# Start addresses and block sizes of the moving operands in a two-chunk encoder layer

## The chip, the cores and the metric

The kernel runs on one core of a Trainium2 chip. The metric is the device time of one launch in microseconds; the median of the runs counts. The core's engines are called as in the profile: PE (TensorE, with PEld for its weight loads), DVE (VectorE), ACT (ScalarE), POOL (GpSimd) and SP (SyncE, which here issues every DMA).

## What is computed

One layer of a hybrid encoder is applied to two sequences, a prompt of 1024 tokens and a sample of 256. Sixteen meta tokens stand ahead of each. The model width is 2048, and a head has 128 numbers. Cut to what matters:

```python
def encoder_layer(h, ...):                       # h: meta tokens, then the sequence
    u = rms_norm(h, norm_w) @ w_in               # 2048 -> 6656 = 52 strips of 128
    qa, ka, va, za, qb, kb, vb, zb = split(u)
    qa, ka = rope(rms_norm(qa)), rope(rms_norm(ka))
    ya = global_gqa(qa, ka, va) * silu(za)       # 8 heads, 2 key heads, all tokens
    qb, kb = rms_norm(qb), rms_norm(kb)
    yb = neighbourhood_attention(qb, kb, vb, rpb) * silu(zb)   # 8 heads, local windows + meta keys
    return h + concat([ya, yb]) @ w_out          # 2048 -> 2048

y_prompt, y_sample = encode(x_prompt), encode(x_sample)        # without the meta rows
```

Everything is float32.

## The kernel before

**Operands.** Each float32 operand of a projection is split into a rounded half h (float32r) and the remainder l. A product then takes three matmuls: wh with xh, wh with xl, wl with xh. Weights are the stationary operand (128x128), tokens are the moving one. A tile of moving tokens has shape `[P, 2, T]`: h in `t[:, 0, :]`, l right behind it in `t[:, 1, :]`.

**Two chunks of tokens.** Chunk 1 holds T1 = 512 tokens: 16 meta tokens, the 256 of the sample, and the first C1P = 240 of the prompt, in this order. Chunk 2 holds the T2 = 784 other prompt tokens. For each chunk, 52 strips of `w_in` (128 output columns each) are multiplied with 16 k-tiles of tokens (`strips`, lines 196 to 198). A strip of chunk 1 is one block: all 512 tokens for k and v (`B0`), and 496 for q and z (`BQ`), which need no meta tokens and so start at token 16. A strip of chunk 2 is two blocks of 392 tokens (`BL`, line 662).

**Around the strips.** After each strip an evacuation reads PSUM: `qk_evac` (norm, rope and split), `z_evac` (silu), or `v_rows` with `rows_out`, where TensorE turns v to token-major form, 128 tokens at a time, ACT copies it and SP stores it. Attention is interleaved: `attend` (L318 to 320 and L358 to 361) for global heads, `attend_sample` and `attend_strip` for local ones. k, v, q and z of chunk 1's prompt part pass through DRAM (`kd`, `vn`, `qd`, `zd`) and are loaded in chunk 2. A scheduler sets the order of instructions when the kernel is built; DMAs all go through SP's queue.

**Out projection.** `outproj` multiplies `w_out` with TH = 640 columns at a time, in seven products instead of eight, formed from sums of operand quarters. Each is two blocks of 320 columns of a tile `ym`, shape `[P, 2, 640]` (`products`, lines 913 to 915).

**Memory.** A DMA scratch of 16384 bytes a partition stands at the bottom of SBUF, below the kernel's tiles. The tiles x and ym start at 96 past a multiple of 128 bytes. A second half starts 2048 bytes behind the first in chunk 1, 3136 in chunk 2 and 2560 in the out projection; the second block starts 1568 bytes in (chunk 2) or 1280 (out projection).

Of the kernel before, what the change touches and what calls it, by code (L numbers as in the profile page):

```python
# [20 lines left out]
P = 128  # L21
# [8 lines left out]
T2 = NP - C1P  # L30
NH = 8
# [14 lines left out]
class Kern:  # L46
# [88 lines left out]
    def load_all_x(self):  # L135


        nc = self.nc
        t = [self.x.tile([P, 2, T2], F32R, tag="x", name="x") for _ in range(KT)]
        for kt, i in enumerate((3, 4, 0, 1, 2, *range(5, KT))):  # L140
            h, l = t[i][:, 0, :], t[i][:, 1, :]
            r = l.bitcast(F32)
            with self.tc.issue_after(self.early):
                nc.sync.dma_start(r, self.x2d[kt][:])
            w = self.nw[:, kt:kt + 1]
            nc.scalar.activation(h, r, AF.Copy, scale=w)
# [217 lines left out]
    def attend_sample(self, q, zs, k, meta, vals, vmeta, tab, ydst):  # L364
# [123 lines left out]
    def copy_km(self, k):  # L488

        km = self.k.tile([P, 2, 3, NMETA], F32R, tag="km", name="km")  # L490
        self.nc.scalar.copy(km[:], k[:, :, :NMETA].bitcast(F32).unsqueeze(2).to_broadcast([P, 2, 3, NMETA]))
        km = km[:].rearrange("p i c m -> p i (c m)")
        return km[:, 0], km[:, 1]
# [58 lines left out]
    def chunk1(self):  # L552
# [21 lines left out]

        def v_strip(s, g):
# [4 lines left out]
            def evac(ps):  # L580
                vt = self.v_rows(ps[0], *B0)
                self.split(vm[:, 0:1, :], vm[:, 1:2, :], self.v_turn(vt, [0], NMETA))
                if loc:
                    nc.scalar.copy(vs[:], self.v_turn(vt, [NMETA + 32 * w0 for w0 in WIN0]))
                else:
                    self.split(vs[:, :2, :], vs[:, 2:, :], self.v_turn(vt, [NMETA, NMETA + P]))
                self.rows_out(vt[:, PS:], C1P, self.vn[g], 0)
# [5 lines left out]
        def q_strip(s, h, wc, rope):  # L593
            q = self.s.tile([P, 2, QB], F32R, tag="S", name="qs")

            def evac(ps):
                o, n = BQ
                qp = [self.ev.tile([P, C1P], F32R, tag="ev", name="qp") for _ in range(2)]
                self.qk_evac(ps[0], o, n, wc, (ct[:, o:], st[:, o:]) if rope else None,
# [16 lines left out]
        def run(h, q, z, k, v, vm, tab):  # L616
# [5 lines left out]
            o = NMETA  # L622
            keys = [(k[:, 0, o + P * j:o + P * j + P], k[:, 1, o + P * j:o + P * j + P]) for j in range(2)]
# [29 lines left out]
    def chunk2(self):  # L653
# [8 lines left out]
        BL = [(0, T2 // 2), (T2 // 2, T2 // 2)]  # L662
# [3 lines left out]
        def k_first(g):  # L666
            k = self.k.tile([P, 2, NMETA + NP], F32R, tag="k1", name="kf")
            nc.sync.dma_start(k[:, :, :K0].bitcast(F32), self.kd[g][:])
            return k, self.copy_km(k)
# [169 lines left out]
    def y_load(self, p, k):  # L839
# [6 lines left out]
        if p in (1, 2, 4):  # L846
            t = self.ym.tile([P, 2, TH], F32R, tag="ym", name="ym")
# [5 lines left out]
    def y_operand(self, p, k, r):  # L853
# [11 lines left out]
        t = self.ym.tile([P, 2, TH], F32R, tag="ym", name="ym")  # L865
# [23 lines left out]
    def x_load(self, p, s):  # L889
# [6 lines left out]
        if half == 0:  # L896
            nc.sync.dma_start(o[:, :C1P], io["x1"][:, c, NMETA + NS:])
            nc.sync.dma_start(o[:, C1P:], io["x2"][:, c, :TH - C1P])
        else:
            nc.sync.dma_start(o[:, :NP - TH], io["x2"][:, c, TH - C1P:])  # L900
            nc.sync.dma_start(o[:, NP - TH:], io["x1"][:, c, NMETA:NMETA + NS])
# [114 lines left out]
    def build(self):  # L1016
# [3 lines left out]
        with tc.tile_pool(name="dr", bufs=1, space=DRAM) as dp, tc.tile_pool(name="const", bufs=1) as cp, \  # L1020
# [17 lines left out]
            with ExitStack() as ps, ExitStack() as es_y:  # L1038
# [6 lines left out]
                kw = {"reuse_waits": "tile"}  # L1045
                pool(es_one, "one2", 1, side="right")
# [44 lines left out]
def _constants():  # L1091
# [3 lines left out]
    rows = np.concatenate([np.full(NMETA, -1), rs, rp]).astype(np.float32)  # L1095
    cols = np.concatenate([np.arange(NMETA), cs, cp]).astype(np.float32)
# [55 lines left out]
```

## Time and profile before

| | |
|---|---|
| time, median of 3 runs | 2222.65 us (2222.65 to 2224.98) |
| span of the profiled execution | 2221.7 us |
| granted TensorE clock, mean over the span | 1.000 |
| DMA | 391.21 MB, 176 GB/s on average, 55.1% of 16 engines' span |

The profile names a group of instructions by line, engine, operation, and tiles (out<-in); "128x392" is partitions by columns of the moving operand. A matmul's duration runs from its first column in to its last result out, so successive ones overlap, and the distance from start to start tells what one costs. Rows of stretches give, for each engine, busy time and number of instructions, then the granted TensorE clock, the DMA share and GB/s. Rows of the timeline begin with start and duration in us. In the waits of an engine, a row has the total in us, the number of times and the longest.

### The profile page before, as it was taken

How to read it: one execution, taken by the hardware profiler on the slowest of the kernel's cores; microseconds unless marked ns; L12 is line 12 of the kernel's file. 1: busy time of each engine (PE TensorE's matmuls, PEld its weight loads, DVE VectorE, ACT ScalarE, POOL GpSimd, SP SyncE). 2: the span in 40 equal slices, each digit the busy share in tenths (PEclk: the TensorE clock that was granted, in tenths of full speed). 3: DMA queues.
4: the chain of work that ended last, by engine and by line, in shares of the span. 5: the costliest groups of instructions: out<-in, count | busy, mean ns of one | idle time of the engine just before them, and what ended most of it. 6: DMA issues, size and time to landing. Idle time of an engine off the chain costs nothing.

```text
span 2221.7 us, 36835 instructions
## 1 busy us (share of the span) xinstructions
PE 2200.6 (99%) x13074; PEld 2088.6 (94%) x13074; DVE 1639.8 (74%) x2895; ACT 1128.1 (51%) x2298; POOL 525.3 (24%) x249
## 2 busy tenths in 40 slices
PE   8999999999999999999999999999999999999999
PEld 7888788888889999999999999999999999999999
DVE  7687876787864898986898988767768776536743
ACT  6555454454554666665666666444445454232220
POOL 1232421122302232321233233423323312000000
PEclk9999999999999999999999999999999999999999
DMA  8767899998555333334333336644343464745663
GB/s 298 216 193 223 275 305 307 322 298 285 166 207 152 99 106 114 103 104 147 96 113 111 101 113 190 180 151 136 111 128 120 137 233 136 242 139 162 206 208 111
DMA packets 267480, 391.21 MB, mean 176 GB/s; under 512 B 46720, under 2 KB 126496, under 8 KB 267296
## 3 DMA queue, kind: packets, MB, share of 16 engines
q1 hardware_dynamic: 267296, 388.86, 55.1%
q8 instruction: 102, 1.67, 0.3%
q14 instruction: 82, 0.67, 0.1%
HBM read 286.19 MB, written 102.42 MB: 175 GB/s over the span
## 4 chain that ended last, share of the span: by engine, by line
PE 91%; DVE 3%; DMA 3%; issue 1%; ACT 1%; POOL 1%; SPq 0%; DVEq 0%; ACTq 0%; POOLq 0%
PE pp L196 20%; PE pp L197 20%; PE pp L198 20%; PE pq L914 6%; PE pq L915 6%; PE pq L913 6%; PE po L457 2%; PE sp L318 1%; PE sp L320 1%; PE sp L319 1%; PE po L360 1%; PE po L359 1%; PE po L358 1%; DVE wl L53 1%; DMA wld<-wl 1%
## 5 line engine op out<-in xcount | busy, mean ns | idle before, releaser
L196 PE MATMUL pp<-x,wh 128*128 128x392 f32 (+2 forms) x2496 | 893.7, 359 | 5.9 <-ACT wh L52 5.6
L197 PE MATMUL pp<-x,wh 128*128 128x392 f32 (+2 forms) x2496 | 893.4, 358 | 0.7 <-DVE x L147 0.7
L198 PE MATMUL pp<-x,wl 128*128 128x392 f32 (+2 forms) x2496 | 891.0, 357 | 0.2 <-DVE wl L53 0.2
L196 PEld LDWEIGHTS pp<-x,wh 128*128 128x128 f32 x2496 | 469.1, 188 | 39.5 <-ACT wh L52 7.0
L198 PEld LDWEIGHTS pp<-x,wl 128*128 128x128 f32 x2496 | 469.3, 188 | 33.2 <-DVE wl L53 1.2
L197 PEld LDWEIGHTS pp<-x,wh 128*128 128x128 f32 x2496 | 469.5, 188 | 32.7 <-DVE x L147 1.0
L53 DVE TENSOR_TENSOR wl<-wr,wh 128x512 fp32r<-128x512 f32 (+1 forms) x402 | 285.3, 722 | 136.1 <-ACT wh L52 113.8
L52 ACT CAST wh<-wr 128x512 fp32r<-128x512 f32 (+1 forms) x402 | 239.8, 610 | 233.7 <-PE pp L197 166.5
L206 POOL PARTITION_ALL_REDUCE m<-ms x78 | 226.5, 2904 | 395.7 <-ACT ms L204 377.6
L287 POOL PARTITION_ALL_REDUCE tot<-a x80 | 187.9, 2349 | 465.3 <-DVE a L285 454.7
L914 PE MATMUL pq<-ym,wh 128*128 128x320 f32 x896 | 277.6, 310 | 2.8 <-DVE ym L53 2.8
L915 PE MATMUL pq<-ym,wl 128*128 128x320 f32 x896 | 277.1, 309 | 0.2 <-DVE wl L53 0.2
L913 PE MATMUL pq<-ym,wh 128*128 128x320 f32 x896 | 276.8, 309 | 0.0
L270 POOL PARTITION_ALL_REDUCE ma<-m x80 | 101.0, 1262 | 443.5 <-DVE m L268 434.3
L914 PEld LDWEIGHTS pq<-ym,wh 128*128 128x128 f32 x896 | 168.3, 188 | 3.8 <-DVE ym L53 3.8
L915 PEld LDWEIGHTS pq<-ym,wl 128*128 128x128 f32 x896 | 168.3, 188 | 0.5 <-DVE wl L53 0.5
L913 PEld LDWEIGHTS pq<-ym,wh 128*128 128x128 f32 x896 | 168.3, 188 | 0.3 <-ACT ym L52 0.2
L338 DVE TENSOR_TENSOR S<-S,ma 128x512 f32<-128x512 f32 x136 | 105.4, 831 | 8.8 <-POOL ma L270 8.5
L53 DVE TENSOR_TENSOR pl<-S,ph 128x512 fp32r<-128x512 f32 x136 | 97.5, 723 | 13.9 <-ACT ph L52 13.5
L322 ACT COPY S<-sp 128x512 f32<-128x512 f32 x136 | 78.0, 578 | 52.9 <-PE sp L320 40.5
L339 ACT ACTIVATE S<-S 128x512 f32<-128x512 f32 x136 | 83.9, 629 | 40.2 <-DVE S L338 39.7
L181 ACT CAST wh<-wr 128x512 fp32r<-128x512 f32 x132 | 81.2, 615 | 39.1 <-PE pp L197 38.5
(207 smaller groups left out, 3310.3 us busy)
## 6 DMA issues: line engine op xcount, KB each, us to landing
wr<-in_w_in SPq DMA_DIRECT2D x414, 256.0 KB
wld<-wl SPq DMA_DIRECT2D x132, 256.0 KB
wl<-wld SPq DMA_DIRECT2D x132, 256.0 KB
wq<-in_w_out SPq DMA_DIRECT2D x64, 256.0 KB
td<-wq SPq DMA_DIRECT2D x64, 256.0 KB
wr<-td SPq DMA_DIRECT2D x64, 256.0 KB
yr<-yd SPq DMA_DIRECT2D x48, 320.0 KB
wr<-in_w_out SPq DMA_DIRECT2D x48, 256.0 KB
```

Source lines behind the costliest of these rows:

```text
L52: self.hi = nc.scalar.copy(hi, full).ins
L53: return nc.vector.tensor_tensor(out=lo, in0=full, in1=hi.bitcast(F32), op=ALU.subtract).ins
L196: nc.tensor.matmul(p[:, :n], wh[:, k, :], xh[:, o:o + n], start=first, stop=False)
L197: nc.tensor.matmul(p[:, :n], wh[:, k, :], xl[:, o:o + n], start=False, stop=False)
L198: nc.tensor.matmul(p[:, :n], wl[:, k, :], xh[:, o:o + n], start=False, stop=last)
L206: nc.gpsimd.partition_all_reduce(m2[:], ms[:], P, RED.add)
L270: nc.gpsimd.partition_all_reduce(ma[:], m1[:], P, RED.max)
L287: nc.gpsimd.partition_all_reduce(tot[:], a1[:], P, RED.add)
L338: nc.vector.tensor_tensor(out=s, in0=s, in1=mb, op=ALU.subtract)
L913: nc.tensor.matmul(ps[:, b, :B], wh, yh[:, o], start=k == 0, stop=False)
L914: nc.tensor.matmul(ps[:, b, :B], wh, yl[:, o], start=False, stop=False)
L915: nc.tensor.matmul(ps[:, b, :B], wl, yh[:, o], start=False, stop=k == 7)
```

## The change

- The moving tiles x (both chunks) and ym are allocated at multiples of 128 bytes (`align_bytes=ALIGN`), with a pad of 96 bytes on the right side of SBUF.
- In chunk 2 the tile x is 800 columns wide instead of 784, so the second half starts 3200 bytes in; the two blocks have 384 and 400 tokens, so the second block starts 1536 bytes in.
- In chunk 1 the meta tokens stand last, behind sample and prompt. q and z blocks of 496 tokens start at token 0 instead of 16. The rope tables, the input `x1`, the slices for k, v and the residual follow.
- The DMA scratch is cut to 4096 bytes a partition.

```diff
+TX = 800
+NB = 384
+ALIGN = 128
...
-            t = self.x.tile([P, 2, T1], F32R, tag="x", name="x")
+            t = self.x.tile([P, 2, T1], F32R, tag="x", name="x", align_bytes=ALIGN)
...
-        t = [self.x.tile([P, 2, T2], F32R, tag="x", name="x") for _ in range(KT)]
+        t = [self.x.tile([P, 2, TX], F32R, tag="x", name="x", align_bytes=ALIGN) for _ in range(KT)]
...
-            h, l = t[i][:, 0, :], t[i][:, 1, :]
+            h, l = t[i][:, 0, :T2], t[i][:, 1, :T2]
...
-            o, c = NMETA + 32 * w0, slice(64 * w, 64 * w + 64)
+            o, c = 32 * w0, slice(64 * w, 64 * w + 64)
...
-        B0, BQ = (0, T1), (NMETA, NS + C1P)
-        PS = NMETA + NS
+        B0, BQ = (0, T1), (0, NS + C1P)
+        PM = NS + C1P
...
-                nc.sync.dma_start(self.kd[g][:, :, :NMETA], kt_[:, :, :NMETA].bitcast(F32))
-                nc.sync.dma_start(self.kd[g][:, :, NMETA:], kt_[:, :, PS:].bitcast(F32))
-                return kt_, self.copy_km(kt_)
+                nc.sync.dma_start(self.kd[g][:, :, :NMETA], kt_[:, :, PM:].bitcast(F32))
+                nc.sync.dma_start(self.kd[g][:, :, NMETA:], kt_[:, :, NS:PM].bitcast(F32))
+                return kt_, self.copy_km(kt_[:, :, PM:])
...
-                self.rows_out(vt[:, PS:], C1P, self.vn[g], 0)
+                self.rows_out(vt[:, NS:PM], C1P, self.vn[g], 0)
...
-        BL = [(0, T2 // 2), (T2 // 2, T2 // 2)]
+        BL = [(0, NB), (NB, T2 - NB)]
...
-            t = self.ym.tile([P, 2, TH], F32R, tag="ym", name="ym")
+            t = self.ym.tile([P, 2, TH], F32R, tag="ym", name="ym", align_bytes=ALIGN)
...
+                pool(ps, "pad", 1, side="right")
+                self.pad.tile([P, 24], F32, name="pad")
...
-    x = np.concatenate([a["meta"], a["x_sample"][0][gs], a["x_prompt"][0][gp]])
+    xp = a["x_prompt"][0][gp]
+    x = np.concatenate([a["x_sample"][0][gs], xp[:C1P], a["meta"], xp[C1P:]])
...
-    nc = bacc.Bacc("TRN2", target_bir_lowering=False, num_devices=1)
+    nc = bacc.Bacc("TRN2", target_bir_lowering=False, num_devices=1, dynamic_dma_scratch_size=4096)
```

More of the change, by code (lines that the diff above doesn't have):

```diff
@@ L490, in copy_km @@
         km = self.k.tile([P, 2, 3, NMETA], F32R, tag="km", name="km")
-        self.nc.scalar.copy(km[:], k[:, :, :NMETA].bitcast(F32).unsqueeze(2).to_broadcast([P, 2, 3, NMETA]))
+        self.nc.scalar.copy(km[:], k.bitcast(F32).unsqueeze(2).to_broadcast([P, 2, 3, NMETA]))
         km = km[:].rearrange("p i c m -> p i (c m)")
@@ L581, in evac @@
                 vt = self.v_rows(ps[0], *B0)
-                self.split(vm[:, 0:1, :], vm[:, 1:2, :], self.v_turn(vt, [0], NMETA))
+                self.split(vm[:, 0:1, :], vm[:, 1:2, :], self.v_turn(vt, [PM], NMETA))
                 if loc:
-                    nc.scalar.copy(vs[:], self.v_turn(vt, [NMETA + 32 * w0 for w0 in WIN0]))
+                    nc.scalar.copy(vs[:], self.v_turn(vt, [32 * w0 for w0 in WIN0]))
                 else:
-                    self.split(vs[:, :2, :], vs[:, 2:, :], self.v_turn(vt, [NMETA, NMETA + P]))
-                self.rows_out(vt[:, PS:], C1P, self.vn[g], 0)
+                    self.split(vs[:, :2, :], vs[:, 2:, :], self.v_turn(vt, [0, P]))
+                self.rows_out(vt[:, NS:PM], C1P, self.vn[g], 0)
                 for i, j in enumerate((0, 1, 0)):
@@ L598, in evac @@
                 qp = [self.ev.tile([P, C1P], F32R, tag="ev", name="qp") for _ in range(2)]
-                self.qk_evac(ps[0], o, n, wc, (ct[:, o:], st[:, o:]) if rope else None,
+                self.qk_evac(ps[0], o, n, wc, (ct[:, o:o + n], st[:, o:o + n]) if rope else None,
                              [(0, NS, q[:, 0, :], q[:, 1, :]), (NS, C1P, qp[0][:], qp[1][:])])
@@ L621, in run @@
                 return
-            o = NMETA
-            keys = [(k[:, 0, o + P * j:o + P * j + P], k[:, 1, o + P * j:o + P * j + P]) for j in range(2)]
+            keys = [(k[:, 0, P * j:P * j + P], k[:, 1, P * j:P * j + P]) for j in range(2)]
             self.attend(q, z[:], keys, km, [(v[:, j, :], v[:, 2 + j, :]) for j in range(2)], vm[:], ydst)
@@ L668, in k_first @@
             nc.sync.dma_start(k[:, :, :K0].bitcast(F32), self.kd[g][:])
-            return k, self.copy_km(k)
+            return k, self.copy_km(k[:, :, :NMETA])
         def k_strip(s, g, wc, rope):
@@ L896, in x_load @@
         if half == 0:
-            nc.sync.dma_start(o[:, :C1P], io["x1"][:, c, NMETA + NS:])
+            nc.sync.dma_start(o[:, :C1P], io["x1"][:, c, NS:NS + C1P])
             nc.sync.dma_start(o[:, C1P:], io["x2"][:, c, :TH - C1P])
@@ L900, in x_load @@
             nc.sync.dma_start(o[:, :NP - TH], io["x2"][:, c, TH - C1P:])
-            nc.sync.dma_start(o[:, NP - TH:], io["x1"][:, c, NMETA:NMETA + NS])
+            nc.sync.dma_start(o[:, NP - TH:], io["x1"][:, c, :NS])
         return o
@@ L1094, in _constants @@
     (_, rs, cs), (_, rp, cp) = _grid(NS // 64), _grid(NP // 64)
-    rows = np.concatenate([np.full(NMETA, -1), rs, rp]).astype(np.float32)
-    cols = np.concatenate([np.arange(NMETA), cs, cp]).astype(np.float32)
+    rows = np.concatenate([rs, rp[:C1P], np.full(NMETA, -1), rp[C1P:]]).astype(np.float32)
+    cols = np.concatenate([cs, cp[:C1P], np.arange(NMETA), cp[C1P:]]).astype(np.float32)
     ar = inv[:, None] * rows[None, :]
```

2 lines of the change are left out of this document (1 added, 1 removed).

## The prediction

> **What bounds the kernel now.** I read the page first: busy shares, clock, chain of work. Then TensorE's waits, its groups with shapes kept apart, and stretches of its timeline.
>
> ```profile
> span 2221.7 us, 36835 instructions
> PE 2200.6 (99%) x13074; PEld 2088.6 (94%) x13074; DVE 1639.8 (74%) x2895; ACT 1128.1 (51%) x2298; POOL 525.3 (24%) x249
> PEclk9999999999999999999999999999999999999999
> PE 91%; DVE 3%; DMA 3%; issue 1%; ACT 1%; POOL 1%; SPq 0%; DVEq 0%; ACTq 0%; POOLq 0%
> PE pp L196 20%; PE pp L197 20%; PE pp L198 20%; PE pq L914 6%; PE pq L915 6%; PE pq L913 6%; PE po L457 2%; PE sp L318 1%; PE sp L320 1%; PE sp L319 1%; PE po L360 1%; PE po L359 1%; PE po L358 1%; DVE wl L53 1%; DMA wld<-wl 1%
> ```
>
> TensorE carries 91% of the chain that ended last, at a granted clock of nine tenths or more in every slice. The six lines that the change aims at (196 to 198, 913 to 915) hold 78% of the chain. The waits of TensorE, of which these are the longest three and the shortest, add up to 16.8 us over all eleven rows of that view:
>
> ```profile
> PE pp L196 <- ACT wh L52: 5.6, 2, 5.4
> PE pq L914 <- DVE ym L53: 2.8, 4, 1.3
> PE sp L318 <- ACT qs L52: 2.2, 2, 1.1
> ...
> PE pp L196 <- ACT x L146: 0.2, 1, 0.2
> ```
>
> So 99% of the span is matmuls following one another, and a matmul's spacing is the price of everything. Next, TensorE's groups, shapes apart (busy us, mean ns of one):
>
> ```profile
> L196 PE MATMUL pp<-x,wh 128*128 128x392 f32 x1664 | 568.0, 343 | 0.3 <-ACT x L146 0.2
> L914 PE MATMUL pq<-ym,wh 128*128 128x320 f32 x896 | 277.6, 310 | 2.8 <-DVE ym L53 2.8
> L196 PE MATMUL pp<-x,wh 128*128 128x496 f32 x512 | 198.1, 387 | 0.0
> L196 PE MATMUL pp<-x,wh 128*128 128x512 f32 x320 | 127.8, 401 | 5.6 <-ACT wh L52 5.6
> L320 PE MATMUL sp<-q,kf 128*128 128x256 f32 x256 | 71.8, 282 | 0.0
> L319 PE MATMUL sp<-q,kf 128*128 128x256 f32 x256 | 71.4, 280 | 0.0
> L318 PE MATMUL sp<-q,kf 128*128 128x256 f32 x256 | 70.2, 279 | 0.0
> ```
>
> Each of the first four groups has two sisters of equal count, so the change touches 4992 matmuls of 392 columns, 2688 of 320, 1536 of 496 and 960 of 512. These durations overlap; what counts is the distance from one start to the next. In the out projection TensorE never stops, and I count matmuls:
>
> ```profile
> 1900.00:2200.00 300.00, 300.00 (x2048) 300.00 (x2047) 163.98 (x230) 77.68 (x131) 0.00 (x0) 1.00 0.58 183
> 684.98:713.43 28.45, 28.45 (x161) 28.45 (x161) 10.30 (x16) 14.15 (x29) 5.52 (x2) 1.00 0.49 151
> ```
>
> About 2046 spacings in 300 us give 146.6 ns for 320 columns; 160 in 28.45 us give 177.8 ns for 392 (a stretch of strips alone). Single starts give the other two sizes, and 256 in attention:
>
> ```profile
> 299.89 0.39 PE L198 MATMUL pp<-x,wl 128*128 128x512 f32 x1
> ...
> 301.99 0.39 PE L198 MATMUL pp<-x,wl 128*128 128x512 f32 x1
> ...
> 549.24 0.38 PE L198 MATMUL pp<-x,wl 128*128 128x496 f32 x1
> ...
> 552.59 0.39 PE L198 MATMUL pp<-x,wl 128*128 128x496 f32 x1
> ...
> 1299.53 0.28 PE L318 MATMUL sp<-q,kf 128*128 128x256 f32 x1
> ...
> 1300.12 0.28 PE L320 MATMUL sp<-q,kf 128*128 128x256 f32 x1
> ```
>
> Nine spacings in 2.10 us: 233.3 ns for 512. Fifteen in 3.35 us: 223.3 ns for 496. Five in 0.59 us: 118 ns for 256. All lie at 2.17 to 2.22 columns per ns. The built program gives the start addresses: before, 512 and 320 columns begin 96 bytes past a multiple of 128, 496 begin 32 past, attention's 256 begin on the multiple, and 392 take turns: blocks 0 and 1 of the rounded half at 96 and 0, of the remainder half at 32 and 64.
>
> That mixture is the evidence. In the 28.45 us stretch six matmuls repeat: block 0 thrice (96, 32, 96), block 1 thrice (0, 64, 0). Starts of successive threes in another clean stretch:
>
> ```profile
> 1786.12 0.34 PE L196 MATMUL pp<-x,wh 128*128 128x392 f32 x1
> 1786.66 0.34 PE L196 MATMUL pp<-x,wh 128*128 128x392 f32 x1
> 1787.18 0.34 PE L196 MATMUL pp<-x,wh 128*128 128x392 f32 x1
> 1787.72 0.34 PE L196 MATMUL pp<-x,wh 128*128 128x392 f32 x1
> 1788.25 0.34 PE L196 MATMUL pp<-x,wh 128*128 128x392 f32 x1
> 1788.79 0.34 PE L196 MATMUL pp<-x,wh 128*128 128x392 f32 x1
> ```
>
> Block 0 takes 0.54 us each time, block 1 0.52 and 0.53. Sorting the 159 undisturbed starts of the stretch whose row is above (first and last here) by start address gives mean spacings of 175.0 ns at 0, 177.3 at 32, 179.3 at 64, 180.2 at 96:
>
> ```profile
> 684.98 0.34 PE L196 MATMUL pp<-x,wh 128*128 128x392 f32 x1
> ...
> 713.25 0.34 PE L196 MATMUL pp<-x,wh 128*128 128x392 f32 x1
> ```
>
> Sorting all 4992 by duration, interrupted ones out, gives 338.7, 340.3, 340.5 and 342.1 ns: the same order, smaller steps.
>
> **The change part by part.** *Start addresses.* All four sizes go to 0. By the clean stretch a matmul saves 5.2 ns from 96, 2.3 from 32, and 2.8 for the mean of the 392 (177.8 less 175.0). By all records it is 3.4, 1.6 and 1.7. The out projection is as clean as the stretch, so 2688 x 5.2 = 14.0 us there (9.1 by the other). The strips are interleaved with attention and transposes, so all records: 4992 x 1.7 = 8.5 us (14.0), 960 x 3.4 = 3.3 (5.0), 1536 x 1.6 = 2.5 (3.5). Sum 28.3 us, between 23.4 and 36.5. For the 496, 512 and 320 the step is borrowed from the 392, since no trace has these sizes at 0. It could be nothing there (then 8.5 alone), or more, since in the mixture an aligned matmul follows a late neighbour.
>
> A rule speaks against the size of this. The Trainium skill ("SBUF — State Buffer", section "Specifications (TRN2)") says that reads pay for crossing into a new 16-byte line. All starts, old and new, are multiples of 16, so the count of lines stays and the sum by that rule would be 0. The trace disagrees as far as 392 columns go: 5.2 ns between two starts which that rule treats alike.
>
> *Blocks of 384 and 400 instead of 392.* The columns are the same: half gain and half lose 8. Vector and scalar work per strip is unchanged in sum; in the stretch above DVE was busy 10.30 of 28.45 us and ACT 14.15, so the last block's 8 columns more (2% of an operation) stay hidden. Without that cover a strip's last operations would be late by that 2%. One effect is countable: 392 left 8 rows over in turning v, 384 leaves none. Ten transposes, ten ACT copies and ten small stores on the SP queue vanish. A transpose row stands at 273 ns; four matmuls of 192 columns,
>
> ```profile
> L478 PE MATMUL tp<-ident,vt 128*8 128x128 f32 x20 | 5.5, 273 | 0.0
> 1803.33 0.27 PE L424 MATMUL sp<-q,kf 128*128 128x192 f32 x1
> ...
> 1803.78 0.28 PE L425 MATMUL sp<-q,kf 128*128 128x192 f32 x1
> ```
>
> are 0.45 us apart, 0.11 each, which I take for a small one: 1.1 us saved, at most 2.7.
>
> *Meta tokens last, the pad, 800-column tiles, smaller DMA scratch.* The same copies and transfers with other offsets: nothing on TensorE. The scratch (16384 to 4096 bytes a partition) pays for the longer tiles; every DMA here is issued by SP, so nobody uses it.
>
> *Order.* The schedule is made anew: about a fifth of TensorE's instructions stand elsewhere. No new instruction and no new kind of wait is added; what can move is the 16.8 us of waits. I take no change, with 8 us (half of them) either way. A faster TensorE asks DMA for the same bytes sooner, and chunk 1 is where that is tightest:
>
> ```profile
> 300.00:660.00 360.00, 357.98 (x1718) 301.82 (x1717) 269.81 (x441) 184.03 (x367) 76.63 (x31) 1.00 0.82 273
> ```
>
> At a DMA share of 0.82, chunk 1's gain of 6 us (1%) raises it to 0.83. I leave it whole; at worst those 6 us are lost.
>
> Sum: 28.3 + 1.1 = 29.4 us off 2221.7, 2192.3 in the profile. The median of the runs lies 1 us above that span, so 2193.
>
> **The rivals.** *Nothing but the transposes: 2221.5.* For it: 256 columns, already at 0, run at 2.17 per ns, no better than 320 at 96 with 2.18. Against it: the four steps of the 392. Attention's matmuls are short and its weight loads, 0.11 us apart where little streams, may cover a gain.
>
> *Recovery of the rate: 2147 and below.* If late reads alone hold the stream at 2.2 columns per ns, aligned operands could run faster than any 392 here. The first matmuls show a slow state, 0.43 us for 512:
>
> ```profile
> 7.64 0.63 PE L197 MATMUL pp<-x,wh 128*128 128x512 f32 x1
> 8.07 0.63 PE L198 MATMUL pp<-x,wl 128*128 128x512 f32 x1
> 8.50 0.63 PE L196 MATMUL pp<-x,wh 128*128 128x512 f32 x1
> ```
>
> Twice that rate is 2.4 per ns: 213, 207, 163 and 133 ns for 512, 496, 392 and 320, so 20 + 16.6 + 14.5 + 13.3 ns on their counts: 19 + 25 + 72 + 36 = 152 us, 2070. Half of it, 76 us, gives 2147. Against it: aligned 392s take 175, not 163.
>
> The Trainium skill ("TensorE: Matmul & The Clock Gate", "Wait — 56ns, not 53.3ns?") gives a warm spacing of N/2.4 plus about 2.5 ns and names no start address. For 392 that is 165.8 against 177.8 measured, for 512 215.8 against 233.3; by that rule the sum would be 127 us and 2095.
>
> *Slower: moving and stationary reads collide: 2247.* The stationary tiles of both projections start at 0 as well. In attention, with moving operands at 0, line 320 has its weights at 0 and takes 282 ns; 318 and 319, with weights 64 past, take 279 and 280. If equal starts cost 2.5 ns, the 10176 matmuls pay 25 us from the first matmul on, and the step above was something else. Against it: the 392s at 0 have weights at 0 too and are the cheapest.
>
> **How the numbers follow.** Forecast 0.66; its own range is 2175 to 2221 (below: 36.5 + 8 of waits + 2.7 for transposes; above: the 392s' 8.5 + 1.1, less 8 of waits). Nothing 0.12, half the recovery or more 0.11, collision 0.11. Range 2142 to 2228: it takes in the nothing case and the half recovery, and leaves out what lies beyond that and the collision, just under 0.2. This kernel's measurement tells about 0.2%, 4.4 us, from no change. Faster: forecast, less 0.03 for its upper end, and recovery: 0.74. Same: nothing and those 0.03: 0.15. Slower: collision: 0.11.
>
> **What would show it.** Right: in the out projection 2123 matmuls instead of 2048 in 300 us (141.4 ns), 384 and 400 together near 176 a piece, 512 near 230, waits still near 17 us. Spacings unchanged: nothing gained. All near 2.4 columns per ns: recovery. Spacings longer with the clock at 1.00: collision. Wrong in another way: spacings as forecast, but TensorE's waits up by what they gained.

## The result, and the profile after

The changed kernel takes 2227.65 us in the median of 13 runs (2223.06 to 2233.42), the kernel before 2223.91 (13 runs beside it, 2222.24 to 2226.47). The ratio is 1.002, with a 95% interval of 1.0012 to 1.0028: slightly slower, where 2193 us was forecast. The profiled execution is a long one among the 13, 2232.76 us with a span of 2231.0. Of the page of the changed kernel, the lines that answer to those of before (the strips are now lines 199 to 201, the out projection 915 to 917):

```profile
span 2231.0 us, 36738 instructions
PE 2207.4 (99%) x13064; PEld 2101.0 (94%) x13064; DVE 1644.2 (74%) x2895; ACT 1127.5 (51%) x2288; POOL 531.2 (24%) x249
PE 89%; DVE 4%; DMA 3%; issue 1%; ACT 1%; SPq 1%; POOL 0%; DVEq 0%; ACTq 0%; POOLq 0%
```

The ten transposes are gone (13064 matmuls instead of 13074), and TensorE still is the bound. The forecast's largest term is tested by one stretch of the changed kernel, 300 us of the out projection:

```profile
1900.00:2200.00 300.00, 300.00 (x2047) 300.00 (x2046) 163.88 (x230) 79.40 (x134) 0.00 (x0) 1.00 0.58 186
```

2047 matmuls where 2123 were forecast and 2048 ran before: 320 columns still cost 146.6 ns, though they now start on a multiple of 128 bytes. The other sizes, by first and last starts in the timeline of the changed kernel and one stretch of strips of chunk 2:

```profile
298.70 0.39 PE L200 MATMUL pp<-x,wh 128*128 128x512 f32 x1
...
302.15 0.39 PE L200 MATMUL pp<-x,wh 128*128 128x512 f32 x1
...
548.70 0.39 PE L199 MATMUL pp<-x,wh 128*128 128x496 f32 x1
...
552.50 0.39 PE L201 MATMUL pp<-x,wl 128*128 128x496 f32 x1
...
1018.68 0.34 PE L201 MATMUL pp<-x,wl 128*128 128x384 f32 x1
...
1051.43 0.34 PE L200 MATMUL pp<-x,wh 128*128 128x400 f32 x1
1018.90:1051.50 32.60, 32.60 (x183) 32.60 (x182) 11.02 (x18) 13.89 (x27) 5.37 (x2) 1.00 0.43 137
```

512: 15 spacings in 3.45 us, 230 ns; the longest undisturbed stretches, of 47 and 63 matmuls, run at 227.3 to 227.5 (233.3 and 233.4 before). 496: 17 in 3.80, 223.5 (223.3). 384 and 400: 183 matmuls, 182 spacings in 32.75 us, 179.9 ns, where 392 had 177.8. So the change made the 4992 matmuls of chunk 2 slower. The waits of TensorE, the four longest of 14 rows, which add up to 19.4 us (16.8 before):

```profile
PE pp L199 <- ACT wh L55: 7.0, 2, 5.5
PE sp L321 <- ACT qs L55: 2.4, 2, 1.3
PE pq L916 <- DVE ym L56: 1.9, 2, 1.4
PE po L364 <- DVE Pm L283: 1.7, 4, 0.6
```

And the clock. Three stretches of the changed kernel, in the view by stretches (the last three numbers are granted clock, DMA share, GB/s):

```profile
0.00:20.00 20.00, 12.74 (x37) 8.93 (x38) 12.25 (x25) 14.41 (x29) 2.69 (x9) 0.93 0.83 272
620.00:640.00 20.00, 18.52 (x104) 17.28 (x103) 14.82 (x24) 13.77 (x25) 3.67 (x2) 0.91 0.94 330
1800.00:1900.00 100.00, 95.78 (x629) 93.45 (x628) 68.47 (x134) 46.71 (x91) 19.77 (x10) 0.95 0.60 198
```

and the same three of the kernel before:

```profile
0.00:20.00 20.00, 14.17 (x50) 9.93 (x50) 14.06 (x28) 16.22 (x33) 3.03 (x9) 1.00 0.85 279
620.00:640.00 20.00, 17.98 (x100) 15.90 (x99) 14.54 (x23) 13.07 (x25) 2.85 (x2) 1.00 0.80 267
1800.00:1900.00 100.00, 96.08 (x666) 94.26 (x665) 70.55 (x136) 48.13 (x94) 19.58 (x10) 1.00 0.65 216
```

After short waits of TensorE the clock was granted at half speed for 3.4 or 6.8 us at a time. One such place in the timeline of the changed kernel:

```profile
13.34 0.39 PE L201 MATMUL pp<-x,wl 128*128 128x512 f32 x1
15.24 0.50 PE L199 MATMUL pp<-x,wh 128*128 128x512 f32 x1 [1.52 <-ACT wh L55]
...
18.95 0.63 PE L201 MATMUL pp<-x,wl 128*128 128x512 f32 x1
19.38 0.63 PE L199 MATMUL pp<-x,wh 128*128 128x512 f32 x1
...
20.87 0.40 PE L201 MATMUL pp<-x,wl 128*128 128x512 f32 x1
```

TensorE waits 1.52 us, and 2 us later matmuls are 0.43 us apart instead of 0.23, until 20.6.

To put both spans into one account, I add up the distances from one matmul's start to the next by size, over the whole trace. A distance above 1.12 times its size's median counts as that median, and the rest of it as stall (waits and half-clock stretches). The columns add up to 9.8 us less than the span in both kernels: that much lies ahead of the first matmul and behind the start of the last. In us:

| | 512 | 496 | 392, or 384 and 400 | 320 | 256 | smaller | stall | of it half clock | span |
|---|---|---|---|---|---|---|---|---|---|
| before | 224.0 | 344.2 | 889.9 | 394.1 | 230.2 | 100.6 | 28.9 | 0 | 2221.7 |
| after | 218.7 | 341.5 | 896.7 | 394.1 | 230.5 | 99.8 | 39.8 | 8.5 | 2231.0 |

The sizes below 256 mix several shapes; with one median for each of these sizes, some 6 us pass from "smaller" to "stall" in both rows alike, and the other columns stay. The clock stood at half speed for 17.1 us in four places, and I count half of that, 8.5, as the time lost. The change saved 5.3 + 2.7 + 0.8 us and spent 6.8 on chunk 2 and 0.3 on 256: 1.7 us less in spacings. Stalls took 10.9 us more, 8.5 of them half clock. Over all runs the half clock weighs less than in this one: the mean granted clock is 0.9981 after and 0.9989 to 0.9994 in the sets of runs of the kernel before that have it on record, and 0.001 of 2225 us is 2.2 us. So the 3.7 us between the medians are about 1.7 gained, 2 lost to the clock, and a rest of some 3 that would be waits; the profiled execution shows 2.4 more of these.

### The profile page after: what moved, and what is told of

The parts are those of the page before. It is cut to its first block, busy times and chain, and to the rows that moved or that the text cites. A ratio compares the mean times of both kernels' runs of the same rounds, so it can differ in the third digit from the quotient of the medians.

```text
span 2231.0 us, 36738 instructions
## 1 busy us (share of the span) xinstructions
PE 2207.4 (99%) x13064; PEld 2101.0 (94%) x13064; DVE 1644.2 (74%) x2895; ACT 1127.5 (51%) x2288; POOL 531.2 (24%) x249
## 4 chain that ended last, share of the span: by engine, by line
PE 89%; DVE 4%; DMA 3%; issue 1%; ACT 1%; SPq 1%; POOL 0%; DVEq 0%; ACTq 0%; POOLq 0%
PE pp L199 19%; PE pp L200 19%; PE pp L201 19%; PE pq L916 6%; PE pq L917 6%; PE pq L915 6%; PE po L460 2%; PE sp L321 1%; PE sp L322 1%; PE sp L323 1%; PE po L363 1%; PE po L361 1%; PE po L362 1%; DVE wl L56 1%; PE sp L428 1%
## 5 line engine op out<-in xcount | busy, mean ns | idle before, releaser
L199 PE MATMUL pp<-x,wh 128*128 128x384 f32 (+2 forms) x2496 | 896.3, 360 | 7.0 <-ACT wh L55 7.0
L200 PE MATMUL pp<-x,wh 128*128 128x384 f32 (+2 forms) x2496 | 893.7, 358 | 0.0
L201 PE MATMUL pp<-x,wl 128*128 128x384 f32 (+2 forms) x2496 | 889.3, 356 | 0.2 <-DVE wl L56 0.2
L273 POOL PARTITION_ALL_REDUCE ma<-m x80 | 111.1, 1388 | 421.7 <-DVE m L271 419.1
```

The costliest lines, as they stand in the source:

```text
L199: nc.tensor.matmul(p[:, :n], wh[:, k, :], xh[:, o:o + n], start=first, stop=False)
L200: nc.tensor.matmul(p[:, :n], wh[:, k, :], xl[:, o:o + n], start=False, stop=False)
L201: nc.tensor.matmul(p[:, :n], wl[:, k, :], xh[:, o:o + n], start=False, stop=last)
L273: nc.gpsimd.partition_all_reduce(ma[:], m1[:], P, RED.max)
```

## The experiments

Kernels made of matmul streams alone compute nothing of the layer: they put one layout after another on TensorE, each 16 k-tiles with three matmuls a block, in the order of the strips, with nothing else running. In the lists `CONFIGS` a block is its start and its columns, in elements of 4 bytes.

### 1. One block alone, by start address

```diff
+CONFIGS += [([(f, n)], 0, 0) for n in (256, 320, 384, 392, 400, 496, 512) for f in (0, 8, 16, 24)]
```

> Leaves the layer out: 64 short streams of 48 matmuls (96 with two blocks) back to back, each with its own column count, start address and arrangement, nothing else on the engine. Theory A (start address as I predicted): for 392 columns the spacing grows by about 2 ns with each 32 bytes past a multiple of 128 (175, 177, 179, 180 ns at 0, 32, 64, 96), and 320 and 512 show the same steps. Theory B (only the column count and the order of blocks count): a stream of equal starts costs the same at 0, 32, 64 and 96, within 1 ns, and the 384/400 pair comes out near 359.4 ns, the 392 pair of before near 355.7, as in the two kernels. Theory C (collision of moving and stationary reads): weights 64 bytes past a multiple of 128 take 3 ns or more off at a moving start of 0, and add them at a start of 64.

The timeline has each stream's 48 matmuls in a row; the last matmul's successor begins the next stream. Each row is the start of a stream: 320 columns at 0 and the stream behind it, 320 at 96 and the one behind it, then 392 at 0, 32, 64 and 96 and the one behind them:

```profile
80.54 0.31 PE L1050 MATMUL pp<-xb,wb 128*128 128x320 f32 x1
...
87.58 0.31 PE L1050 MATMUL pp<-xb,wb 128*128 128x320 f32 x1
...
101.70 0.31 PE L1050 MATMUL pp<-xb,wb 128*128 128x320 f32 x1
...
108.76 0.34 PE L1050 MATMUL pp<-xb,wb 128*128 128x384 f32 x1
...
142.42 0.34 PE L1050 MATMUL pp<-xb,wb 128*128 128x392 f32 x1
...
150.96 0.34 PE L1050 MATMUL pp<-xb,wb 128*128 128x392 f32 x1
...
159.59 0.34 PE L1050 MATMUL pp<-xb,wb 128*128 128x392 f32 x1
...
168.07 0.34 PE L1050 MATMUL pp<-xb,wb 128*128 128x392 f32 x1
...
176.81 0.34 PE L1050 MATMUL pp<-xb,wb 128*128 128x400 f32 x1
```

320: 7.04 us at 0 (146.7 ns each) and 7.06 at 96. 392: 8.54, 8.63, 8.48, 8.74 us, so 177.9, 179.8, 176.7 and 182.1 ns at 0, 32, 64 and 96. The order 0, 32, 64, 96 that the forecast rests on isn't there: 64 is the best, and a stream at 0 costs 177.9 and not 175.0. 512 ran at 231.1 (0, 32) and 233.3 (64, 96); the halves stood 3456 bytes apart here and the weights' second tile 2176 bytes behind the first (27 and 17 x 128), which matters below. 384 and 400 took 175.6 and 182.2 at 0. No theory came out whole. With the weights moved by 64 bytes, 392 took 175.6 at 0 and 177.8 at 64, 512 took 233.3 and 231.1, and 320 stayed at 146.7: shifts of up to 2.3 ns in both directions, where the collision theory asked for 3 or more. And the pairs came out in the reverse order of the kernels: 384 and 400 at 177.8, the blocks of 392 with the starts of before at 179.4.

### 2. The layouts of both kernels alone

```diff
+    ([(0, 384), (384, 400)], 1600, 800, *D),
+    ([(24, 392), (416, 392)], 1568, 784, *D),
+CONFIGS += [([(0, 512)], 1600, lo, *D) for lo in (0, 512, 528, 544, 576, 640, 768, 832, 1024)]
```

> Leaves the layer out: streams of 48 or 96 matmuls again, now with the kernels' own layouts (distance between the halves, stride of the tiles, place of the weights) and variations of one of them at a time. Theory D (the spacing is set by where the reads of tokens and weights stand to each other, in a pattern that locks in): the replicas give the kernels' spacings within 0.5 ns (512 columns 227.6 at 0 and 233.3 at 96; 496 columns 222 and 223; the pair 359.4 for 384/400 and 355.7 for 392/392; 320 columns 146.7 at both), and change by 2 to 6 ns when only the distance between the halves or the place of the weights is moved, with the start of the tokens left at 0. Theory A (the start alone): only the start matters, the distance between the halves and the weights' place change nothing within 1 ns. Narrower weights (32, 64, 96 of 128 columns) shorten the spacing if the weight load is what disturbs the stream, by up to 4 ns; unchanged if it isn't. If the spacing is 0.444 ns a column plus some 4 ns a matmul, blocks of 512 and 272 give 353 ns for a pair, 3 less than 392/392.

Two stretches of 14 us, the changed kernel's chunk 2 and then that of before:

```profile
98.00:112.00 14.00, 14.00 (x79) 14.00 (x78) 0.00 (x0) 0.00 (x0) 0.00 (x0) 1.00 0.00 1
115.00:129.00 14.00, 14.00 (x81) 14.00 (x80) 0.00 (x0) 0.00 (x0) 0.00 (x0) 1.00 0.00 1
```

By the starts of the streams that is 180.0 ns a matmul against 177.8, with no other engine at work: the loss in chunk 2 is a matter of TensorE and its operands' places. 320 columns gave 146.7 at 0 and at 96, 512 gave 226.7 at 0 and 233.3 at 96, 496 gave 223.3 both at 0 and at 160, the old place. With 512 at 0, only the distance between the halves was moved: 226.7 at 2048, 2304, 2560, 3072, 3328 and 4096 bytes, 232.1 at 2112, 233.3 at 2176. With the weights' second tile 2176 bytes behind the first, 231.1. So what pays for 512 columns is a multiple of 256 bytes between the operands, not of 128. Two hopes failed: narrower weights (32, 64 and 96 columns) gave 177.8 for 392 and 230.0 to 231.5 for 512, and only 320 with weights of 32 got shorter, 143.3; and 512 ahead of 272 took 178.8 a matmul and not 176.5.

### 3. Parts of the change, in the kernel

First the changed kernel with two blocks of 392 again:

```diff
-NB = 384
+NB = 392
```

> The changed kernel with blocks of 392 and 392 again, so starts in chunk 2 are 0 and 32 in both halves. If the sizes 384 and 400 are what costs: the pair of blocks falls from 359.4 to 355.7 ns or below (175.0 + 177.3 = 352.3 if the steps seen before hold), 9 to 18 us less than the changed kernel, 2218 to 2209 in time. If a start at 0 in all matmuls is what costs: the pair stays near 359 and the time near 2227.

The changed kernel with all of chunk 2 as before (blocks of 392, halves 3136 bytes apart, a start at 96):

```diff
-NB = 384
+NB = 392
...
-        t = [self.x.tile([P, 2, TX], F32R, tag="x", name="x", align_bytes=ALIGN) for _ in range(KT)]
+        t = [self.x.tile([P, 2 * TX], F32R, tag="x", name="x", align_bytes=ALIGN) for _ in range(KT)]
...
-            h, l = t[i][:, 0, :T2], t[i][:, 1, :T2]
+            h, l = t[i][:, 24:24 + T2], t[i][:, 24 + T2:24 + 2 * T2]
```

> The changed kernel with chunk 2 as before: blocks of 392 that start at 96 and 0 in the rounded half, 32 and 64 in the remainder half. Both theories: the pair is 355.7 ns again, chunk 1 keeps 227.6 ns for 512 and 222.1 for 496, the out projection 146.7 ns. That is 9 us less of spacings than the changed kernel and 8 less than before: 2216 if the waits are as before (29 us of excess over the spacings), 2221 if the waits stay as in the profile of the changed kernel (40 us), which would put 5 us or more of the loss on waits.

The kernel before with the new order of tokens alone, so that 496 start at 96 and all else stays:

```diff
-        B0, BQ = (0, T1), (NMETA, NS + C1P)
+        B0, BQ = (0, T1), (0, NS + C1P)
...
```

> Only the order of chunk 1's tokens is changed, meta tokens last; all tiles lie as before, so the blocks of 496 begin at 96 instead of 32. If the start sets the spacing as the streams measured alone show it (226.7 against 222.2 ns), 1536 x 3 to 4.5 ns are lost: 2228 to 2230. If the order of tokens costs waits of its own, the excess over the spacings rises above the 29 us of before, as it did in the three kernels that have it (34 to 40 us); if it does not, it stays at 29 to 31.

The kernel before with the new chunk 2 alone (and the scratch that makes room for it):

```diff
-        t = [self.x.tile([P, 2, T2], F32R, tag="x", name="x") for _ in range(KT)]
+        t = [self.x.tile([P, 2, 800], F32R, tag="x", name="x", align_bytes=128) for _ in range(KT)]
...
-        BL = [(0, T2 // 2), (T2 // 2, T2 // 2)]
+        BL = [(0, 384), (384, 400)]
```

> The kernel before with chunk 2 of the changed one alone: tiles at a multiple of 128, halves 3200 bytes apart, blocks of 384 and 400 (and the small DMA scratch that pays for it). The spacings must lose what the profile of the changed kernel shows, 6.8 us in 4992 matmuls: 2229 to 2231 with waits as before. By my prediction it would gain 8.5 to 14 us: 2210 to 2215. If the loss in the changed kernel came from elsewhere, it stays at 2223.

The kernel before with the smaller scratch alone:

```diff
-    nc = bacc.Bacc("TRN2", target_bir_lowering=False, num_devices=1)
+    nc = bacc.Bacc("TRN2", target_bir_lowering=False, num_devices=1, dynamic_dma_scratch_size=4096)
```

> The kernel before with the smaller DMA scratch alone (4096 bytes a partition instead of 16384); every start stays at the same place past a multiple of 128. All four kernels with it show three or two stretches of half clock in their profiles and a mean clock of 0.998, the two without it one at the very end and 0.999. If the scratch or the layout it shifts is what costs these: 2226 to 2229, clock 0.998, excess over the spacings 34 or more. If it is harmless: the time of before within 1 us, excess near 29.

Medians of 9 or more runs, the median of the kernel before on the same chip, the ratio to it (medians compare within a row only), and the account of the profiled execution:

| | median | before beside it | ratio, 95% interval | chunk 2's spacings | 512 + 496 | stall | half clock |
|---|---|---|---|---|---|---|---|
| before | 2223.91 | | 1 | 889.9 | 568.2 | 28.9 | 0 |
| after | 2227.65 | 2223.91 | 1.0020 (1.0012 to 1.0028) | 896.7 | 560.2 | 39.8 | 8.5 |
| e1_nb392 | 2225.88 | 2223.39 | 1.0009 (1.0000 to 1.0017) | 893.3 | | 36.4 | 5.1 |
| e2_chunk2_old | 2223.12 | 2223.39 | 0.9999 (0.9990 to 1.0008) | 891.4 | | 33.9 | 3.4 |
| f2_meta_last | 2225.30 | 2225.53 | 0.9996 (0.9988 to 1.0004) | | 496: 345.2 | 28.7 | 0 |
| f3_chunk2_alone | 2232.21 | 2225.53 | 1.0025 (1.0015 to 1.0035) | 896.7 | | 34.5 | 5.1 |
| f1_scratch | 2227.45 | 2225.23 | 1.0006 (0.9997 to 1.0015) | | | 32.9 | 3.4 |

Chunk 2's part alone makes the kernel 0.25% slower, with the same 896.7 us of spacings as in the changed kernel; taken back (e2), the rest of the change is worth nothing that can be told from none, though it has 8.0 us less on 512 and 496: its stalls are 5.0 us longer, 3.4 of them half clock, and chunk 2 runs 1.5 us longer than before, with some stretches at 177.9 ns and others at 178.9. e1 divides the loss: with 392 at the new places chunk 2 takes 893.3 us, so 3.4 of the 6.8 come with the sizes and as much with the places. The order of tokens alone does nothing that can be told from none either (4.6 to 6.9 us of loss were expected from the streams; its spacings of 496 grew by 1.0). The scratch stays open: its interval holds 1, and its mean clock over the runs was 0.9984 against 0.9991 for the kernel before beside it.

### 4. Chunk 1's part alone, and the half clock

The first kernel, g1, is f2_meta_last with a pad of 96 bytes ahead of chunk 1's x, so that 496 and 512 start at 0, and all else as before.

```diff
+                    pool(es_1, "pad", 1, side="right")
```

> Of the change only what chunk 1 needs: meta tokens last and a pad of 96 bytes during chunk 1, so that 512 and 496 columns begin at a multiple of 128; chunk 2, out projection and DMA scratch as before. Spacings: 512 columns 227.6 ns, 496 columns 222.1 ns, the rest as before, 8 us less than before. If the spacings of chunk 1 carry through to the end: ratio 0.996 to 0.997 of before. If chunk 1 loses them in waits for its transfers whatever the scratch is: ratio 0.999 to 1.000, as with chunk 2 as before and the small scratch.

The next two have 40 added matmuls on zeros, which go into no output, put where TensorE had waited (14 ahead of chunk 2's first strip, 14 and 12 ahead of two products of the out projection): h1 in the changed kernel, h2 in g1.

```diff
+            if self.second and self.fresh:
+                self.fresh = False
+                self.busy(out[0][0][:, :QB], 14)
...
+    def busy(self, out, n):
+        for _ in range(n):
+            self.nc.tensor.matmul(out, self.dz[:, :P], self.dz[:], start=True, stop=True)
...
-            ps = self.products(ws.pop(n), [ys[8 * (n // 8) + k] for k in range(8)])
+            ps = self.products(ws.pop(n), [ys[8 * (n // 8) + k] for k in range(8)], {0: 14, 8: 12}.get(n, 0))
```

> The changed kernel with 40 matmuls of 256 columns on a tile of zeros (1.7, 1.7 and 1.4 us) put where TensorE waited and its clock then halved: before the first strip of chunk 2, before the out projection and before its second product. Their results are overwritten. If the stretches of half clock come from the waits just ahead of them: those near 625, 1812 and 1894 us are gone, the mean clock rises from 0.998 to 0.999, and 3 to 5 us are won, 2223 to 2225. If they don't depend on the waits: the stretches stay, and up to 5 us are added, 2228 to 2233.

> Chunk 1's part of the change alone (meta tokens last, tiles of chunk 1 at a multiple of 128) with the same 40 matmuls, which need 1 KB and so a DMA scratch of 14336 bytes. If the half clock after waits ate what chunk 1 gained: 2 us below the kernel without them, 2220 or ratio 0.997 to 0.9975. If not: 2222 to 2226.

g1 took 2222.56 us, 0.9985 (0.9975 to 0.9995) of before: the only version whose whole interval lies below the kernel before. Its account: 512 at 218.6 and 496 at 341.3, 8.3 us less in all spacings than before, and 7.2 us more of stalls (1.7 of them half clock). Among its waits is one that the kernel before doesn't have, on a transfer; the third row of this fence:

```profile
PE sp L321 <- ACT qs L55: 2.4, 2, 1.3
PE tp L241 <- DVE vm L56: 2.3, 2, 1.6
PE po L397 <- DMA vm<-vmd: 1.5, 1, 1.5
```

h1 took 2228.61 us, 1.0026 (1.0016 to 1.0036); h2 2220.91, 0.9992 (0.9983 to 1.0000), no better a ratio than g1's. The clock of h1, in the stretches shown above for the changed kernel:

```profile
0.00:20.00 20.00, 14.40 (x46) 10.21 (x47) 13.39 (x27) 15.36 (x31) 3.21 (x10) 1.00 0.82 273
620.00:640.00 20.00, 17.62 (x107) 16.40 (x107) 15.59 (x26) 14.36 (x26) 2.86 (x2) 1.00 0.96 351
1800.00:1900.00 100.00, 97.10 (x679) 96.09 (x678) 69.49 (x135) 47.04 (x91) 19.83 (x10) 1.00 0.61 206
```

Kept busy, TensorE has its full clock in the last two stretches (the first has no added matmul ahead of it; the half clock is there in some of these kernels and not in others). Its mean clock over the runs is 0.9998, where the changed kernel has 0.9981; that is 3.8 us of 2227. The added matmuls cost 4.7 us by the account, so the time didn't gain.

The length of a wait doesn't tell whether the half clock follows. In all eleven traces of whole layers the clock changes only in steps of 3.413 us (or multiples), counted from the first record of it. Cut into such steps, 14 of the 16 half-clock stretches between the start and the last matmul follow a step in which TensorE stood idle for 1.45 us or more, all its waits together; two follow one with 1.07 and 1.22; and no whole step between the first record and the last matmul with more than 1.38 was left without one. The kernel before and f3_chunk2_alone (f3) have the same two waits near 628 us, of 1.07 and 0.69 or 0.70 us. In the kernel before a step ends inside the first; in f3 both fall into one step. The first row is the kernel before, the other two are f3:

```profile
627.11:630.51 3.40, 2.08 (x10) 1.51 (x11) 3.22 (x7) 2.37 (x3) 1.06 (x1) 1.00 0.91 276
627.56:630.97 3.41, 1.65 (x12) 1.11 (x12) 2.20 (x7) 2.08 (x5) 0.80 (x1) 1.00 0.81 293
630.98:634.38 3.40, 3.40 (x11) 2.99 (x11) 3.00 (x5) 1.54 (x3) 0.26 (x1) 0.50 0.95 300
```

TensorE was busy for 2.08 us of the step in the one, and the clock stayed; for 1.65 in the other, and it halved. So where the steps fall seems to decide, and that differs from trace to trace; in the kernel before no step from the first record to the last matmul holds more than 1.33 us of idle time, in h1 none more than 1.02. No run moved the steps alone.

### 5. Which layouts are fast, and what decides

```diff
+for a, b in ((384, 400), (400, 384), (392, 392)):
+    for gap in (416, 448) if a > 384 else (384, 416, 448):
+        for lo in (832, 864, 896):
+            CONFIGS.append(([(0, a), (gap, b)], 1792, lo, *D))
+CONFIGS += [([(o, n)], 1792, 896, *D) for n in (384, 400, 496, 512) for o in (0, 32, 64)]
```

> Streams of matmuls alone, as in the two spacing studies before, now with many places of the second block (1536, 1664 or 1792 bytes behind the first), of the second half (3328, 3456 or 3584 bytes, or block by block) and of the weights' second tile. Theory 'even multiples': 512 columns are at their fastest, 226.7 ns, only where halves and weights stand at multiples of 256 bytes to each other, and the same holds for the pair of blocks in chunk 2; then some layout with 1536 or 1792 and 3328 or 3584 runs a pair at under 176 ns a matmul, and those with an odd multiple (1664, 3456) at 178 to 180. Rival 'patterns that lock': the pair's spacing follows no such rule; all layouts lie between 177 and 181 ns, none under 177, and the replica of the changed kernel (384 and 400, 1536 and 3200) is again at 180.0 and that of the kernel before again at 177.8. For single blocks of 512 that start at 128 bytes the theory says about 231 (odd against the weights), for 256 bytes 226.7; 496 stay at 222 to 224 in both.

Single blocks follow the multiple of 256: starting at 0, 128 and 256 bytes, 512 take 226.7, 233.3, 226.7 ns, 496 take 223.3, 226.7, 223.3, 400 take 180.0, 183.3, 180.0 and 384 take 173.3, 175.9, 173.3. The pair with the second block 1536 bytes in ran at 176.7 with halves 3328 bytes apart (26 x 128), at 180.0 with 3456 (27 x 128) and again at 180.0 with the changed kernel's 3200 (25 x 128). Two stretches of 15 us, 3328 and then 3456:

```profile
57.00:72.00 15.00, 15.00 (x86) 15.00 (x86) 0.00 (x0) 0.23 (x1) 0.00 (x0) 1.00 0.00 0
74.00:89.00 15.00, 15.00 (x85) 15.00 (x84) 0.00 (x0) 0.00 (x0) 0.00 (x0) 1.00 0.00 1
```

It is no rule for all: 400 ahead of 384 gave 178.9 to 181.2 at seven of eight places, whichever multiples they were, one of them a layout that had run at 177.8 in the second study; with the second block 1664 bytes in, 384 and 400 took 178.9 at both even distances and 177.8 at the odd one; and no pair of 784 columns came under 176. The weights count too: at the changed kernel's 3200 bytes, moving their second tile by 128 bytes off a multiple of 256 took the pair from 180.0 to 177.8. So the changed kernel was run with one number changed.

```diff
-TX = 800
+TX = 832
```

> The changed kernel with one size changed: the tile of chunk 2 is 832 columns wide instead of 800, so that the second half stands 3328 bytes (26 x 128) behind the first instead of 3200 (25 x 128). Theory 'even multiples of 128': as in the streams alone, 384 and 400 fall from 180.0 to 176.7 ns a matmul (their sum in the trace from 896.7 us to about 880), 4992 x 3.3 ns = 16.6 us, so about 2211 us, 0.994 to 0.996 of the kernel before. Rival 'locked pattern': the streams' figure doesn't carry over to strips that attention and transposes interrupt, the sum stays above 893 us and the time between 2222 and 2230. Second rival 'given back': the spacings fall, but waits and half-clock stretches rise with them; the sum of 384 and 400 is near 880 and the time still above 2218.

2224.44 us, 1.0010 (1.0001 to 1.0019), chunk 2's spacings 891.9 us: neither the 880 of the one theory nor the 896.7 of the other. The trace says why. Of its 17 longest undisturbed stretches of chunk 2, ten run at 176.7 ns and seven at 181.1 to 181.4; in the changed kernel all 17 run at 179.7 to 180.0, in the kernel before all 16 at 177.7 to 178.0. Two stretches of 11 us in this kernel, in the same layout:

```profile
1492.00:1503.00 11.00, 11.00 (x62) 10.91 (x61) 9.21 (x19) 6.08 (x13) 4.34 (x4) 1.00 0.19 66
1513.00:1524.00 11.00, 11.00 (x64) 11.00 (x63) 7.50 (x14) 6.21 (x13) 3.67 (x2) 1.00 0.54 199
```

62 matmuls in one and 64 in the other. Last, each stream behind one or two short matmuls of 16 to 256 columns, which shift the moment at which it begins:

```diff
+CONFIGS += [(*A, *D, (q,)) for q in range(16, 272, 16)]
+CONFIGS += [(*A, *D, (q, q)) for q in (128, 192, 208, 224, 240, 256)]
+CONFIGS += [(*c, *D, (q,)) for c in (B, C, E, F) for q in (16, 48, 80, 112, 144, 208)]
```

> Streams alone, each behind one or two matmuls of 16 to 256 columns that shift the moment at which it begins. Theory 'entry decides': the pair of 384 and 400 with 3328 bytes between the halves has two lasting patterns, 176.7 and about 181.3 ns a matmul, and some of the 24 streams with it fall into each; the layouts for which the kernels show one value only stay at it behind all six shifts: 180.0 (3200 bytes), 177.8 (392, the kernel before), 226.7 (512 at 0), 146.7 (320). Rival 'the weights' or the product's place decides': all streams with that layout run at 176.7 and the shift does nothing; what makes the slow pattern in the kernel is then something that the streams don't have.

The short matmul (line 1042) marks where a stream begins:

```profile
141.94 0.21 PE L1042 MATMUL pp<-xb,wb 128*128 128x96 f32 x1
...
159.02 0.21 PE L1042 MATMUL pp<-xb,wb 128*128 128x112 f32 x1
...
176.52 0.22 PE L1042 MATMUL pp<-xb,wb 128*128 128x128 f32 x1
...
435.90 0.17 PE L1042 MATMUL pp<-xb,wb 128*128 128x16 f32 x1
...
453.28 0.19 PE L1042 MATMUL pp<-xb,wb 128*128 128x48 f32 x1
...
540.16 0.17 PE L1042 MATMUL pp<-xb,wb 128*128 128x16 f32 x1
...
557.33 0.18 PE L1042 MATMUL pp<-xb,wb 128*128 128x48 f32 x1
```

The first two streams are the same 96 matmuls of k1's layout: 17.08 us behind 96 columns, 17.50 behind 112. From start to start the fast one repeats 173, 173, 174, 180, 180, 180 ns, mean 176.7; the slow one 172, 169, 177, 192, 184, 192 and 173, 168, 178, 191, 185, 192, mean 181.1. Of the 24 streams of this layout 16 stayed in the fast pattern and eight in the slow one, each to its end; of the six behind two equal matmuls, five in the slow one. The same 64 columns gave a fast stream early on and a slow one at the end, so the width of what stands ahead doesn't decide by itself; what does is open. The other layouts that were tried have one pattern behind all six shifts: 180.0 for the changed kernel's 3200 bytes (17.38 us above, with the short matmul), 177.8 for that of before (17.17), 226.7 for 512 at 0, 146.7 for 320, in six of six streams each.

## Why the prediction was wrong

**The bound** was right: spacings of matmuls, by size, and the 9.8 us at the ends account for all but 29 us of the span before and 40 after.

**The price of a start address** is the step that failed: "by the clean stretch a matmul saves 5.2 ns from 96, 2.3 from 32, and 2.8 for the mean of the 392". The sorted spacings were right as numbers, but they are parts of one repeating pattern: with the kernel before's layout alone, twelve starts in a row are 181, 176, 181, 176, 180, 172, 180, 177, 180, 178, 179 and 173 ns apart, and only the sum, 12 x 177.8, is a property of the layout. In that round matmuls that start at the same 0 are 172 to 173 ns from the next in one place and 176 to 178 in another, so the start doesn't set the spacing. Take the other starts away, and a stream of 392 at 0 costs 177.9, not 175.0 (177.3 to 178.9 with seven other distances of the halves). The text named the doubt ("in the mixture an aligned matmul follows a late neighbour") and drew the wrong sign from it. What the runs showed in place of 5.2 and 2.8 ns saved: nothing for 320, 2.1 ns lost for the pair of chunk 2.

- Out projection: 14.0 us forecast, 0.0 measured (394.1 in both accounts). This term alone is 14 of the 35 us by which the forecast missed, and it was borrowed from the 392. Its rival, "nothing but the transposes", argued from 256 columns at 0 with 2.17 columns per ns, and was right for this size.
- Chunk 2: 8.5 us forecast, 6.8 lost. Blocks of 384 and 400 were taken as the same columns at a better place. Alone they cost 173.3 and 180.0, 176.7 in the mean; with the halves 25 x 128 bytes apart the pair locks at 180.0. At 26 x 128 the streams gave 176.7, but k1 shows that the kernel reaches it in part of its stretches only.
- 512: 3.3 forecast, 5.3 measured. The sign was right, for another reason: the 227.3 to 227.5 ns fit a tile that begins at a multiple of 256, as in the streams (its place beyond the 128 is on no record). 496: 2.5 and 2.7, by luck: the streams give 223.3 at the old place and the new one. Some 0.9 us of what was won lies in three stretches of 91 to 93 matmuls that ran 3.3 ns faster, two of them at 226.7 before and 223.4 after; the rest isn't traced.
- Transposes: 1.1 forecast; the smaller matmuls together take 0.8 us less.
- Waits: "I take no change, with 8 us (half of them) either way". The rows went from 16.8 to 19.4 us, within that. What the forecast didn't have is the half clock behind a wait, 8.5 us in the profiled execution and about 2 us over all runs. That it goes when TensorE is kept busy was shown by h1. Why waits of the same length leave the clock alone in the kernel before is argued above from where the steps of the clock fall, and not shown by a run.
- "I leave it whole; at worst those 6 us are lost", on chunk 1: it was most of that. g1 saved 8.3 us of spacings and 3.3 of time (1.1 to 5.6 by its interval).

**The collision rival** (moving and stationary reads at equal places, 25 us) had the right sign of the result and the wrong mechanism: 512 with both at 0 are the fastest there are. Where tokens and weights stand to each other does matter, by up to 4.4 ns for 512 (226.7 to 231.1), but equal places are no penalty as such.

**The page's rule** that was weighed: "SBUF — State Buffer", "Specifications (TRN2)", of the Trainium skill, by which starts that are multiples of 16 bytes cost alike. It gave 0 for this change's addresses and came nearer to the time than the forecast did, but the runs don't bear it out: 512 columns take 226.7 ns at 0 and 233.3 at 96 or 128.

## What to carry to other kernels

A spacing that depends on an address inside a mixed stream isn't the price of that address: the stream locks into a repeating pattern, and only the mean of a whole round can be carried over, and only to the same layout. Before moving operands in a kernel, run the new layout's stream by itself, with the real distances between halves, blocks and weights and with a few different beginnings. For single blocks, as here the 512 columns, ask for multiples of 256 bytes rather than 128. And don't count a gain of under 1% on TensorE in full where transfers or short waits stand close: here 3.3 of 8.3 us arrived.

## What the runs showed of the hardware

- For 512 columns of float32r, 256 bytes are the unit: 226.7 ns where tokens, halves and weights (of 128 columns) stand at multiples of 256 to each other, 228.9 to 233.3 elsewhere. 320 columns hardly care (146.7 to 147.8).
- One layout can have two lasting patterns, 176.7 and 181.1 ns. A stream keeps the one it falls into at its beginning; what picks it is open. The one kernel with such a layout, k1, ran as a mixture.
- No stream came near 2.4 columns per ns: 320 at 143.3 at best (weights of 32 columns; 146.7 with 128), 392 at 175.6, 512 at 226.7, so 2.26 at most. "TensorE: Matmul & The Clock Gate" of the Trainium skill, section "Wait — 56ns, not 53.3ns?", gives N/2.4 plus 2.5 ns, 215.8 for 512; these operands don't reach it in any run here.
- The half clock comes in stretches of 3.4 or 6.8 us, behind waits of at most 1.7 us, which sum to 1.07 to 2.08 us within 3.413 us.
- In the half-clock stretch shown above 512 columns are 0.43 us apart, 1.2 columns per ns. That is also the pace of the first matmuls (the rows at 7.64 to 8.50 in the prediction), although the stretch of 0 to 20 us reads 1.00: the kernel before's trace has no record of the clock ahead of 9.29 us, and there the stretch counts as full. In all eleven traces of whole layers the first record stands between 9.0 and 11.6 us, and the spacing drops from 427 ns to some 235 at that moment.
